# Grouping the intra-chunk levels of a gated linear attention differently in a two-layer trunk

## The chip, the cores and the metric

The kernel runs on one core of one Trainium2 chip. A core has a matrix engine (TensorE; in the profile PE, with its weight loads as PEld), three other compute engines (VectorE, DVE; ScalarE, ACT; GpSimd, POOL) and a queue engine for transfers (SyncE, SP). Each engine works through its own instructions in order, and semaphores tie the engines together. The metric is the time of one execution in microseconds (us) on the device.

## The reference, cut to what matters

The program is a trunk of two layers over 256 tokens of width 2048, all in fp32. The even layer runs two mixers side by side, HGRN2 (a gated linear recurrence with a 128 x 128 state per head, eight heads) and a gated recurrence (RG-LRU); the odd layer is an mLSTM. Each layer ends with a gated embedding. The change touches only HGRN2:

```python
w = exp(where(causal, b[:, :, :, None, :] - b[:, :, None, :, :], -inf))   # b = cumsum(log f)
attn = einsum('bhtd,bhsd,bhtsd->bhts', qc, kc, w)
o = einsum('bhtd,bhde->bhte', qc * exp(b), state) + einsum('bhts,bhse->bhte', attn, vc)
new_state = exp(b_last) * state + einsum('bhsd,bhse->bhde', kc * exp(b_last - b), vc)
```

The score of query t and key s is a sum over d of q, k and the product of all forget gates f between s and t.

## The kernel before, in words

**The frame.** The time goes into projections: the activations stand in SBUF, feature by token, split into a high and a low fp32r part (tiles "ahl" in a pool "ap" of 12 buffers), and the weights stream in from HBM. `load_half` loads 128 x 1024 weights into "raw" (5 buffers), ScalarE casts them to "whi" (line 134), VectorE subtracts to "wlo" (line 135), four buffers each. `part_tok` uses two such halves: 24 matmuls of 128 x 512, 12 for each half of the tokens, three for each block of 128 x 128 (lines 164, 165, 166: whi by high, wlo by high, whi by low). Four parts make one projection of 512 columns (`project_tok`), whose sums stand in the PSUM pool "pm", three banks.

**What sets the order.** Everything else is written as generators in lanes. In the middle of each part, after its first 12 matmuls, `pump` takes one step of every lane, and what a step issues is placed behind the matmuls issued so far; the casts and subtractions of weights have a raised priority, so that the scheduler places them ahead. One step of the attention thus comes in each part.

**The attention (`attention(g)`, two groups of four heads).** The scores in a chunk of 32 tokens are built by levels B = 1, 2, 4, 8, 16: at level B the keys of the left half of each block of 2B tokens meet the queries of the right half, each already multiplied by the gates between it and the middle. `scale(B, ...)` takes keys and queries from level B to level 2B: the right queries times the left block's total gate (line 554), the left keys times the right block's total (line 555), and the totals of the next level (line 560). The other two halves stay as they are: where the output is another tile, ScalarE copies them (lines 557, 558); where it is the same tile nothing is to be done. `level(B, ...)` issues 32 matmuls of 32 columns by 16 into a bank of the PSUM pool "px" (tag "mx", three banks), and `keep(B, ...)` writes the valid ones into C by a masked copy on VectorE (line 573). C begins as the diagonal's product (lines 582 and 586).

The steps of a group before: scaled query qf; then diagonal and level 1, and scaling 1 in place; scaling 2 into the tiles k2 and q2; levels 2 and 4, and scaling 4 in place; scaling 8 back into k and qf; levels 8 and 16; scaling 16 in place with the factors of the pairs (64 and 128 tokens); the pairs of 32 and 64 in 48 matmuls (line 642), those of 128 in four (line 647), and all of C and the pairs copied into A by ScalarE (lines 651, 652 and 654); then `read_out`, which multiplies A with the values (lines 675, 678).

Of the kernel before, what the change touches and what calls it, by code (L numbers as in the profile page):

```python
# [11 lines left out]
F32 = mybir.dt.float32  # L12
# [32 lines left out]
def trunk(ctx: ExitStack, tc: tile.TileContext, a, out):  # L45
# [433 lines left out]
    if True:  # L479
# [50 lines left out]
        def attention(g):  # L530
# [10 lines left out]
            k2 = m0.tile([P, 1024], F32, name="k2", tag="k2", bufs=1)  # L541
            q2 = m0.tile([P, 1024], F32, name="q2", tag="q2", bufs=1)
            tot = [f]

            def sides(x, B):
                x = x.rearrange("p (n two b) -> p n two b", two=2, b=B)
                return x[:, :, 0, :], x[:, :, 1, :]

            def scale(B, ko, qo, ki, qi):

                n = 512 // B
                tv = tot[0].rearrange("p (n two) -> p n two", two=2)
                (k0, k1), (q0, q1), (kl, kr), (ql, qr) = (sides(x, B) for x in (ko, qo, ki, qi))
                v.tensor_tensor(out=q1, in0=qr, in1=tv[:, :, 0:1].to_broadcast([P, n, B]), op=ALU.mult)
                v.tensor_tensor(out=k0, in0=kl, in1=tv[:, :, 1:2].to_broadcast([P, n, B]), op=ALU.mult)
                if ko is not ki:
                    s.copy(q0, ql)
                    s.copy(k1, kr)
# [5 lines left out]
            def level(B, ps, at, kk, qq):  # L564
                for c in range(8):
                    for x in range(0, P, 32):
                        o = c * P + x
                        te.matmul(at(ps, c)[x:x + 32], kk[:, o:o + 32], sides(qq[:, o:o + 32], B)[1],  # L568
                                  start=True, stop=True)

            def keep(B, src, cs=slice(0, 8)):
                n = cs.stop - cs.start
                v.copy_predicated(
                    C[:, cs].rearrange("p c (n two b) -> p c n two b", two=2, b=B)[:, :, :, 1, :],
                    lmask[B].rearrange("p (n b) -> p n b", b=B).unsqueeze(1).to_broadcast([P, n, 16 // B, B]),
                    src)

            ps = px.tile([P, 512], F32, name="mx", tag="mx")
            for c in range(8):
                for x in range(0, P, 32):  # L580
                    o = c * P + x
                    te.matmul(ps[x:x + 32, 256 + c * 32:288 + c * 32], k[:, o:o + 32], q[:, o:o + 32],
                              start=True, stop=True)
            level(1, ps, lambda ps, c: ps[:, c * 16:(c + 1) * 16], k, qf)
            t1 = scale(1, k, qf, k, qf)
            v.tensor_tensor(out=C, in0=ps[:, 256:512].rearrange("p (c t) -> p c t", c=8),
                            in1=ident32.unsqueeze(1).to_broadcast([P, 8, 32]), op=ALU.mult)
            keep(1, ps[:, 0:128].rearrange("p (c n b) -> p c n b", c=8, b=1))
            yield
            scale(2, k2, q2, k, qf)  # L590
            yield
            for a_, b_ in ((2, 4), (8, 16)):
                (ka, qa), (kb, qb) = ((k, qf), (k2, q2)) if a_ == 2 else ((k2, q2), (k, qf))
                ps = px.tile([P, 512], F32, name="mx", tag="mx")
# [12 lines left out]
            tot = tot[0]  # L607
# [8 lines left out]
            for i in (1, 0):  # L616
# [7 lines left out]
            k5 = k.rearrange("p (h two b s) -> p h two b s", two=2, b=4, s=32)  # L624
            q5 = qf.rearrange("p (h two b s) -> p h two b s", two=2, b=4, s=32)
            v.tensor_tensor(out=k64, in0=k4[:, :, 0], in1=tb[:, :, 1:2].to_broadcast([P, 8, 32]), op=ALU.mult)
# [684 lines left out]
```

## Time and profile before

| what | value |
|---|---|
| median of 3 runs | 1042.88 us |
| lowest and highest of them | 1041.94 and 1043.24 us |
| the profiled execution's own time | 1041.8 us |
| its span | 1040.0 us |
| mean granted TensorE clock | 0.997 |
| TensorE, matmuls | 1028.8 us, 99% of the span |
| VectorE | 716.6 us, 69% |
| ScalarE | 596.6 us, 57% |

All times of the trace count from the span's start and come from the one profiled execution. A row of a timeline gives start and duration in us, engine, line, operation, output and inputs, shape, and in brackets the idle time of that engine ahead of it with what ended it. Matmuls are pipelined: a row's duration overlaps with the next, so that the distance of two starts, not the duration, is what one costs. An fp32 matmul leaves two records.

### The profile page before, as it was taken

Reading aid. Unit: us, or ns where it says so; the run is one execution under the profiler, and the core shown is the slowest. Engines: PE = TensorE matmul, PEld = TensorE weight load, DVE = VectorE, ACT = ScalarE, POOL = GpSimd, SP = SyncE. Lnnn points to the kernel's source line nnn. Section 1 sums busy time; section 2 is a strip of 40 time slices with the busy share of each in tenths; the row PEclk is TensorE's granted clock in tenths of the full one; section 3 lists DMA queues with packets and bytes.
Section 4 is the critical chain, followed back from the end, with each engine's and each line's share of the span. In section 5 each row is a group of like instructions: output and inputs, shape, how many; then the busy total and the mean of one; then the engine's idle time right before and its main releaser. Section 6 shows DMA issues by size and latency. Waiting matters only on the chain.

```text
span 1040.0 us, 15509 instructions
## 1 busy us (share of the span) xinstructions
PE 1028.8 (99%) x5710; PEld 861.6 (83%) x5710; DVE 716.6 (69%) x1056; ACT 596.6 (57%) x907; POOL 157.0 (15%) x289
## 2 busy tenths in 40 slices
PE   9999999999999999999999999999999999999996
PEld 7888888888878888888889888888888888888886
DVE  6757766779876666777555658885656777666675
ACT  7665565577894354555544656866444654344553
POOL 0020110211222221032000112200001121221120
PEclk9999999999999999999999999999999999999998
DMA  9887664667788787697655678665468887787652
GB/s 339 323 270 241 216 206 164 218 189 222 243 276 260 238 264 236 205 264 258 208 189 192 224 227 263 209 211 169 167 201 229 256 270 237 222 268 239 202 183 81
DMA packets 69036, 236.02 MB, mean 227 GB/s; under 512 B 10328, under 2 KB 10720, under 8 KB 68960
## 3 DMA queue, kind: packets, MB, share of 16 engines
q1 hardware_dynamic: 55584, 197.26, 57.8%
q0 software_dynamic: 13376, 37.77, 13.4%
q8 instruction: 44, 0.72, 0.3%
q14 instruction: 32, 0.26, 0.1%
HBM read 217.16 MB, written 17.83 MB: 226 GB/s over the span
## 4 chain that ended last, share of the span: by engine, by line
PE 95%; DMA 2%; ACT 1%; DVE 0%; SPq 0%; issue 0%; DVEq 0%; ACTq 0%
PE mm L164 29%; PE mm L165 29%; PE mm L166 29%; DMA xq<-in_xT_dram 2%; PE mm L205 1%; PE mm L203 1%; PE mm L204 1%; PE mm L1164 1%; PE mm L1163 1%; PE mm L1162 1%; PE mx L568 1%; PE st L1089 0%; PE st L1088 0%; PE st L1090 0%; PE mx L675 0%; PE mx L996 0%
## 5 line engine op out<-in xcount | busy, mean ns | idle before, releaser
L135 DVE TENSOR_TENSOR wlo<-raw,whi 128x1024 fp32r<-128x1024 f32 (+2 forms) x366 | 444.2, 1220 | 253.4 <-ACT whi L134 240.9
L134 ACT CAST whi<-raw 128x1024 fp32r<-128x1024 f32 (+2 forms) x366 | 381.2, 1045 | 302.0 <-PE mm L166 253.1
L164 PE MATMUL mm<-whi,ahl 128*128 128x512 f32 x1344 | 524.2, 390 | 0.5 <-ACT uz L808 0.5
L165 PE MATMUL mm<-wlo,ahl 128*128 128x512 f32 x1344 | 523.4, 389 | 0.2
L166 PE MATMUL mm<-whi,ahl 128*128 128x512 f32 x1344 | 523.2, 389 | 0.0
L164 PEld LDWEIGHTS mm<-whi,ahl 128*128 128x128 f32 x1344 | 252.3, 188 | 52.9 <-ACT uz L808 1.0
L165 PEld LDWEIGHTS mm<-wlo,ahl 128*128 128x128 f32 x1344 | 252.3, 188 | 52.7 <-DVE wlo L135 1.2
L166 PEld LDWEIGHTS mm<-whi,ahl 128*128 128x128 f32 x1344 | 252.3, 188 | 52.7
L397 POOL DMA_DIRECT2D turned<-zt x96 | 55.5, 607 | 339.6 <-DVE zt L394 250.6
L400 POOL DMA_DIRECT2D zt<-turned x48 | 23.7, 514 | 57.2 <-DMA turned<-zt 44.5
L866 DVE SCALAR_TENSOR_TENSOR qk<-zt,prm,qk 128x255 f32<-128x255 f32 (+2 forms) x48 | 20.9, 474 | 0.7 <-ACT qk L863 0.5
L1080 POOL DMA_DIRECT2D pnr<-in_rows_dram x4 | 2.3, 566 | 125.6 <-DVE pl L1092 97.6
L247 ACT CAST ahl<-zt 128x256 fp32r<-128x256 f32 x32 | 11.7, 402 | 12.0 <-DMA zt<-turned 12.0
L205 PE MATMUL mm<-whi,ahl 128*128 128x256 f32 (+1 forms) x64 | 18.3, 287 | 0.0
L203 PE MATMUL mm<-whi,ahl 128*128 128x256 f32 (+1 forms) x64 | 18.2, 285 | 0.0
L204 PE MATMUL mm<-wlo,ahl 128*128 128x256 f32 (+1 forms) x64 | 18.2, 285 | 0.0
L1163 PE MATMUL mm<-wlo,ahl 128*128 128x256 f32 x64 | 18.1, 283 | 0.0
L1164 PE MATMUL mm<-whi,ahl 128*128 128x256 f32 x64 | 18.1, 283 | 0.0
L1162 PE MATMUL mm<-whi,ahl 128*128 128x256 f32 x64 | 18.1, 283 | 0.0
L248 DVE TENSOR_TENSOR ahl<-zt,ahl 128x256 fp32r<-128x256 f32 x32 | 12.3, 415 | 7.7 <-ACT ahl L247 7.7
L1150 POOL TENSOR_TENSOR pl<-pl,row 128x512 f32<-128x512 f32 x6 | 10.2, 1712 | 46.8 <-ACT sq L1138 46.8
L394 DVE STREAM_TRANSPOSE zt<-hq 128x512 f32<-128x512 f32 x24 | 17.0, 707 | 0.4
(309 smaller groups left out, 832.6 us busy)
## 6 DMA issues: line engine op xcount, KB each, us to landing
raw<-in_ew_dram SPq DMA_DIRECT2D x64, 512.0 KB, 5.0
raw<-in_g_dram SPq DMA_DIRECT2D x56, 512.0 KB, 5.3
raw<-in_eo_dram SPq DMA_DIRECT2D x32, 512.0 KB, 5.4
raw<-in_oqk_dram SPq DMA_DIRECT2D x32, 512.0 KB, 4.6
raw<-in_oog_dram SPq DMA_DIRECT2D x32, 512.0 KB, 4.6
raw<-in_oz_dram SPq DMA_DIRECT2D x32, 512.0 KB, 4.7
raw<-in_oo_dram SPq DMA_DIRECT2D x32, 512.0 KB, 5.4
turned<-zt POOLq DMA_DIRECT2D x96, 128.0 KB, 4.5
```

Of the source, the lines that this page charges most:

```text
L134: last["act"] = s.copy(h, r).ins
L135: last["dve"] = v.tensor_tensor(out=l, in0=r, in1=h.bitcast(F32), op=ALU.subtract).ins
L164: te.matmul(ps[hf], xh, wh, start=(k == 4 * first), stop=False)
L165: te.matmul(ps[hf], xh, wl, start=False, stop=False)
L166: last["pe"] = te.matmul(ps[hf], xl, wh, start=False, stop=(k == 4 * end + 3)).ins
L203: te.matmul(ps[hf], xh, wh, start=(k == 0), stop=False)
L204: te.matmul(ps[hf], xh, wl, start=False, stop=False)
L205: last["pe"] = te.matmul(ps[hf], xl, wh, start=False, stop=(k == KT - 1)).ins
L397: gp.dma_start(out=d.rearrange("i c (x a m) -> i (c x) a m", x=2, a=4)[:, :, k], in_=z[32 * k:32 * k + 32].rearrange("p (b m) -> p b m", b=8))
L1162: te.matmul(ps[hf], xh, wh, start=(k == 0), stop=False)
L1163: te.matmul(ps[hf], xh, wl, start=False, stop=False)
L1164: last["pe"] = te.matmul(ps[hf], xl, wh, start=False, stop=(k == KT - 1)).ins
```

## The change

`scale(B)` always writes into another tile now. The tiles of each level stand in a table `by`: levels 1 and 16 in k and qf, 2 and 32 in k2 and q2, and 4 and 8 in four new tiles of 128 x 1024 in the activations' pool "ahl". The steps become: scaling 1; scaling 2; scaling 4; then the diagonal and levels 1, 2, 4 and 8 one after another into two "mx" banks, with the masked copies of all four and scaling 8; scaling 16; the factors of the pairs; then level 16, its masked copy, and the pairs. The number of steps, matmuls and VectorE instructions is the same; each scaling issues ScalarE's two copies now, ten per group instead of four.

```diff
+            by = {1: (k, qf), 2: (k2, q2), 16: (k, qf), 32: (k2, q2)}
+            for B in (4, 8):
+                by[B] = [ap.tile([P, 1024], F32, name=f"{n}{B}", tag="ahl") for n in "kq"]
...
-            def scale(B, ko, qo, ki, qi):
-
+            def scale(B):
+
+                (ki, qi), (ko, qo) = by[B], by[2 * B]
...
-                if ko is not ki:
-                    s.copy(q0, ql)
-                    s.copy(k1, kr)
+                s.copy(q0, ql)
+                s.copy(k1, kr)
...
-            level(1, ps, lambda ps, c: ps[:, c * 16:(c + 1) * 16], k, qf)
-            t1 = scale(1, k, qf, k, qf)
-            v.tensor_tensor(out=C, in0=ps[:, 256:512].rearrange("p (c t) -> p c t", c=8),
+            scale(1)
+            t1 = tot[0]
+            yield
+            scale(2)
+            yield
+            scale(4)
+            yield
+            ps, p2 = (px.tile([P, 512], F32, name="mx", tag="mx") for _ in range(2))
...
+            found = ((1, ps, 256), (2, ps, 384), (4, p2, 0), (8, p2, 128))
+            for x in found:
+                level(*x)
+            v.tensor_tensor(out=C, in0=ps[:, 0:256].rearrange("p (c t) -> p c t", c=8),
                             in1=ident32.unsqueeze(1).to_broadcast([P, 8, 32]), op=ALU.mult)
-            keep(1, ps[:, 0:128].rearrange("p (c n b) -> p c n b", c=8, b=1))
-            yield
-            scale(2, k2, q2, k, qf)
-            yield
-            for a_, b_ in ((2, 4), (8, 16)):
-                (ka, qa), (kb, qb) = ((k, qf), (k2, q2)) if a_ == 2 else ((k2, q2), (k, qf))
-                ps = px.tile([P, 512], F32, name="mx", tag="mx")
-                level(a_, ps, lambda ps, c: ps[:, c * 16:(c + 1) * 16], ka, qa)
-                level(b_, ps, lambda ps, c: ps[:, 128 + c * 16:144 + c * 16], kb, qb)
-                if b_ == 4:
-                    scale(b_, kb, qb, kb, qb)
-                for i, B in enumerate((a_, b_)):
-                    keep(B, ps[:, i * 128:(i + 1) * 128].rearrange("p (c n b) -> p c n b", c=8, b=B))
-                yield
-                if b_ == 4:
-                    scale(8, ka, qa, kb, qb)
-                    yield
-                else:
-                    scale(b_, kb, qb, kb, qb)
+            for x in found:
+                keep(*x)
+            scale(8)
+            yield
+            scale(16)
+            yield
...
-            k4 = k.rearrange("p (c b s) -> p c b s", b=4, s=32)
-            q4 = qf.rearrange("p (c b s) -> p c b s", b=4, s=32)
+            k4 = k2.rearrange("p (c b s) -> p c b s", b=4, s=32)
+            q4 = q2.rearrange("p (c b s) -> p c b s", b=4, s=32)
...
+            ps = px.tile([P, 512], F32, name="mx", tag="mx")
+            level(16, ps, 0)
+            keep(16, ps, 0)
             banks = []
```

The order of TensorE in the first group before, the three small clumps of levels (mx from q or qf and k; a tile with a number is one of several of its letter, here k2 and q2), with the large matmuls between them left out:

```order
L166 MATMUL mm<-whi,ahl 128x512
L582 MATMUL mx<-q,k 32x32 x32
L568 MATMUL mx<-qf,k 32x16 x32
L164 MATMUL mm<-whi,ahl 128x512
...
L568 MATMUL mx<-qf,k 32x16 x32
L568 MATMUL mx<-q_1082,k_1081 32x16 x32
...
L568 MATMUL mx<-q_1082,k_1081 32x16 x32
L568 MATMUL mx<-qf,k 32x16 x32
```

And now, the one clump, and the beginning of the later one with the pairs (1084 and 1083 are the tiles of level 4, 1086 and 1085 those of level 8):

```order
L166 MATMUL mm<-whi,ahl 128x512
L592 MATMUL mx<-q,k 32x32 x32
L572 MATMUL mx<-qf,k 32x16 x32
L572 MATMUL mx<-q_1082,k_1081 32x16 x32
L572 MATMUL mx<-q_1084,k_1083 32x16 x32
L572 MATMUL mx<-q_1086,k_1085 32x16 x32
L164 MATMUL mm<-whi,ahl 128x512
...
L572 MATMUL mx<-qf,k 32x16 x32
L642 MATMUL mx<-q_1082,k_1081 32x32 x3
```

Three entries from large to small matmuls have become one, and level 16 has joined the entry of the pairs; the one clump stands one part later than the middle one of before stood.

The order of VectorE behind the second clump of the first group, before:

```order
L554 TENSOR_TENSOR q_1082<-q_1082,tot_1206 128x128x4
L555 TENSOR_TENSOR k_1081<-k_1081,tot_1206 128x128x4
L573 COPY_PREDICATED C<-cst,mx 128x64x2
L554 TENSOR_TENSOR qf<-q_1082,tot_1311 128x64x8
L573 COPY_PREDICATED C<-cst,mx 128x32x4
L555 TENSOR_TENSOR k<-k_1081,tot_1311 128x64x8
L135 TENSOR_TENSOR wlo<-raw,whi 128x1024 x2
```

And now, behind the one clump:

```order
L558 TENSOR_TENSOR qf<-q_1086,tot_1187 128x64x8
L559 TENSOR_TENSOR k<-k_1085,tot_1187 128x64x8
L596 TENSOR_TENSOR C<-mx,cst 128x256
L558 TENSOR_TENSOR q_1082<-qf,tot_1396 128x32x16
L576 COPY_PREDICATED C<-cst,mx 128x128
L559 TENSOR_TENSOR k_1081<-k,tot_1396 128x32x16
L576 COPY_PREDICATED C<-cst,mx 128x64x2
L509 TENSOR_SCALAR f<-f,omb,lb 128x256
L576 COPY_PREDICATED C<-cst,mx 128x32x4
L576 COPY_PREDICATED C<-cst,mx 128x16x8
L135 TENSOR_TENSOR wlo<-raw,whi 128x1024 x2
```

The scheduler has drawn scaling 16 up beside scaling 8, so that four products, the diagonal's and four masked copies stand between the clump and the next pair of weight halves; the products of levels 1, 2 and 4 stand ahead of the clump now.

ScalarE in the same place: the copies of scaling 8 and 16 stand in one row, behind the evacuation of a projection (uf) and ahead of the next pair of casts. Before, only the first two of the four were there, between casts.

```order
L498 ACTIVATE uf<-mm,rcr 128x512
L507 ACTIVATE k<-uf 128x256
L508 ACTIVATE f<-uf 128x256
...
L560 COPY qf<-q_1086 128x64x8
L561 COPY k<-k_1085 128x64x8
L560 COPY q_1082<-qf 128x32x16
L561 COPY k_1081<-k 128x32x16
L134 CAST whi<-raw 128x1024 x2
```

The orders of SP and POOL are the same as before.

More of the change, by code (lines that the diff above doesn't have):

```diff
@@ L562, in scale, with level @@
                 return nt
-            def level(B, ps, at, kk, qq):
+            def level(B, ps, at):
+                kk, qq = by[B]
                 for c in range(8):
@@ L567, in level, with keep @@
                         o = c * P + x
[L568 to L572, printed above, removed]
+                        te.matmul(ps[x:x + 32, at + c * 16:at + c * 16 + 16], kk[:, o:o + 32],
+                                  sides(qq[:, o:o + 32], B)[1], start=True, stop=True)
+            def keep(B, ps, at):
                 v.copy_predicated(
-                    C[:, cs].rearrange("p c (n two b) -> p c n two b", two=2, b=B)[:, :, :, 1, :],
-                    lmask[B].rearrange("p (n b) -> p n b", b=B).unsqueeze(1).to_broadcast([P, n, 16 // B, B]),
-                    src)
-            ps = px.tile([P, 512], F32, name="mx", tag="mx")
+                    C.rearrange("p c (n two b) -> p c n two b", two=2, b=B)[:, :, :, 1, :],
+                    lmask[B].rearrange("p (n b) -> p n b", b=B).unsqueeze(1).to_broadcast([P, 8, 16 // B, B]),
+                    ps[:, at:at + 128].rearrange("p (c n b) -> p c n b", c=8, b=B))
+            scale(1)
[6 more added lines that the diff above has]
+            ps, p2 = (px.tile([P, 512], F32, name="mx", tag="mx") for _ in range(2))
             for c in range(8):
@@ L581, in attention @@
                     o = c * P + x
-                    te.matmul(ps[x:x + 32, 256 + c * 32:288 + c * 32], k[:, o:o + 32], q[:, o:o + 32],
-                              start=True, stop=True)
-            level(1, ps, lambda ps, c: ps[:, c * 16:(c + 1) * 16], k, qf)
-            t1 = scale(1, k, qf, k, qf)
-            v.tensor_tensor(out=C, in0=ps[:, 256:512].rearrange("p (c t) -> p c t", c=8),
+                    te.matmul(ps[x:x + 32, c * 32:c * 32 + 32], k[:, o:o + 32], q[:, o:o + 32], start=True, stop=True)
+            found = ((1, ps, 256), (2, ps, 384), (4, p2, 0), (8, p2, 128))
+            for x in found:
+                level(*x)
+            v.tensor_tensor(out=C, in0=ps[:, 0:256].rearrange("p (c t) -> p c t", c=8),
                             in1=ident32.unsqueeze(1).to_broadcast([P, 8, 32]), op=ALU.mult)
-            keep(1, ps[:, 0:128].rearrange("p (c n b) -> p c n b", c=8, b=1))
+            for x in found:
+                keep(*x)
+            scale(8)
             yield
-            scale(2, k2, q2, k, qf)
+            scale(16)
             yield
-            for a_, b_ in ((2, 4), (8, 16)):
-                (ka, qa), (kb, qb) = ((k, qf), (k2, q2)) if a_ == 2 else ((k2, q2), (k, qf))
-                ps = px.tile([P, 512], F32, name="mx", tag="mx")
-                level(a_, ps, lambda ps, c: ps[:, c * 16:(c + 1) * 16], ka, qa)
-                level(b_, ps, lambda ps, c: ps[:, 128 + c * 16:144 + c * 16], kb, qb)
-                if b_ == 4:
-                    scale(b_, kb, qb, kb, qb)
-                for i, B in enumerate((a_, b_)):
-                    keep(B, ps[:, i * 128:(i + 1) * 128].rearrange("p (c n b) -> p c n b", c=8, b=B))
-                yield
-                if b_ == 4:
-                    scale(8, ka, qa, kb, qb)
-                    yield
-                else:
-                    scale(b_, kb, qb, kb, qb)
             tot = tot[0]
@@ L621, in attention @@
             kx, qx = (f[:, i * 512:(i + 1) * 512] for i in range(2))
[L622 to L625 removed]
+            k4 = k2.rearrange("p (c b s) -> p c b s", b=4, s=32)
+            q4 = q2.rearrange("p (c b s) -> p c b s", b=4, s=32)
+            k5 = k2.rearrange("p (h two b s) -> p h two b s", two=2, b=4, s=32)
+            q5 = q2.rearrange("p (h two b s) -> p h two b s", two=2, b=4, s=32)
             v.tensor_tensor(out=k64, in0=k4[:, :, 0], in1=tb[:, :, 1:2].to_broadcast([P, 8, 32]), op=ALU.mult)
```

## The prediction

> **What bounds the kernel now.** I read the page first: busy shares, slices and the chain of waits.
>
> ```profile
> span 1040.0 us, 15509 instructions
> PE 1028.8 (99%) x5710; PEld 861.6 (83%) x5710; DVE 716.6 (69%) x1056; ACT 596.6 (57%) x907; POOL 157.0 (15%) x289
> PE 95%; DMA 2%; ACT 1%; DVE 0%; SPq 0%; issue 0%; DVEq 0%; ACTq 0%
> ```
>
> The chain that ended last is TensorE for 95% of the span. The other engines only matter where TensorE waits for them, so I asked next for TensorE's own waits, over the whole program:
>
> ```profile
> engine line waited for: us in total, times, longest us
> PE st L94 <- POOL ones L91: 1.0, 1, 1.0
> PE mm L164 <- ACT uz L808: 0.5, 1, 0.5
> ```
>
> Two waits, 1.5 us, neither in the attention. So whatever the change does to VectorE and ScalarE is worth nothing unless it makes a new wait on TensorE, and what it can give is TensorE time inside the attention's own stretch (108 to 222 us). The view of the tile "mx" says what is issued there:
>
> ```profile
> L568 PE MATMUL mx<-qf,k x384: 182/183/203, 108.4 to 208.6; 128*32 128x16 f32 x192
> L568 PE MATMUL mx<-q,k x256: 182/183/203, 120.7 to 208.0; 128*32 128x16 f32 x128
> L582 PE MATMUL mx<-q,k x128: 196/196/217, 107.8 to 183.4; 128*32 128x32 f32 x128
>   issue: 2.8, 8
> ...
> L568 PEld LDWEIGHTS mx<-qf,k 128*32 128x32 f32 x384 | 3.9, 108 | 0.7 <-issue 0.7
> ```
>
> The levels' matmuls have 384 + 256 = 640 records, which is 2 groups x 5 levels x 32 x 2: each fp32 matmul leaves two records. They come in clumps between the large matmuls: four per group, eight in all. Eight is also the number of idle pieces of 0.35 us that the view puts down to "issue", that is, to nothing it can name; the last row, from the groups by line, shows that it is the weight loads (PEld) that sat idle so. One clump of the first group, levels 2 and 4, from the timeline of TensorE (start, duration):
>
> ```profile
> 119.37 0.39 PE L164 MATMUL mm<-whi,ahl 128*128 128x512 f32 x1
> 119.59 0.39 PE L165 MATMUL mm<-wlo,ahl 128*128 128x512 f32 x1
> 119.82 0.39 PE L166 MATMUL mm<-whi,ahl 128*128 128x512 f32 x1
> 120.14 0.70 PE L568 MATMUL mx<-qf,k 128*32 128x16 f32 x62
> ...
> 120.71 0.70 PE L568 MATMUL mx<-q,k 128*32 128x16 f32 x62
> 121.34 0.50 PE L164 MATMUL mm<-whi,ahl 128*128 128x512 f32 x1
> 121.67 0.40 PE L165 MATMUL mm<-wlo,ahl 128*128 128x512 f32 x1
> 121.91 0.39 PE L166 MATMUL mm<-whi,ahl 128*128 128x512 f32 x1
> ```
>
> Large matmuls start 0.23 us apart (119.37 to 119.82 is two steps of 0.225, 121.67 to 121.91 one of 0.24). A set of 32 small ones takes 0.57 us from the start of one set to the next (120.14 to 120.71).
>
> **The change part by part.** *TensorE.* Per group it issues the same matmuls: the diagonal's 32, five levels of 32, 48 and 4 of the larger pairs. Only their grouping moves: clumps of (diagonal, 1), (2, 4), (8, 16), (pairs) become (diagonal, 1, 2, 4, 8) and (16, pairs). Two clumps fewer per group, four in all. What does a clump cost beyond its matmuls? From 119.82 to 121.67, the last large matmul before to the second after, are 1.85 us; without the clump they would be two steps, 0.46; the two sets are 1.14. What is left is 1.85 - 0.46 - 1.14 = 0.25 us: 0.09 on the way in (0.32 instead of 0.23), 0.06 in the last set (0.63 instead of 0.57) and 0.10 on the way out (0.33 instead of 0.23). Four clumps fewer: **-1.0 us**. Bounds: nothing at all, if this fixed piece belongs to the sets and comes along with them, and above, if I believe the records' 0.35 us of idle on the way in instead of the 0.09 between starts, 0.35 + 0.16 = 0.51 per clump, 2.0 us. I take 0.25, because the ends of matmuls in this profile are modelled and only the starts are measured.
>
> [...]
>
> *ScalarE and VectorE.* Scaling into other tiles instead of in place adds two ScalarE copies at levels 1, 4 and 16: six per group, twelve in all. The nearest rows are the copies of the levels 2 and 8:
>
> ```profile
> 122.24 0.63 ACT L557 COPY qf<-q 128x512 f32<-128x512 f32 x1 [3.62 <-DVE q L554]
> 122.84 0.63 ACT L558 COPY k<-k 128x512 f32<-128x512 f32 x1
> 123.37 2.12 ACT L134 CAST whi<-raw 128x1024 fp32r<-128x1024 f32 x2
> ```
>
> About 0.6 us each, 12 x 0.6 = 7.2 us of ScalarE. That engine is at 57% and TensorE waits for it once in the program, far from here, so I cost it at nothing, as long as the casts of the weights (whi) and the subtractions (wlo) behind these steps come in time. This is the cover, and I check it where it is thinnest. VectorE's instructions stay the same in number; they move. In the old first clumps VectorE worked behind TensorE; after the second clump (TensorE back at 121.34) it did this:
>
> ```profile
> 121.46 0.69 DVE L554 TENSOR_TENSOR q<-q,tot 128x512 f32<-128x512 f32 x1 [1.44 <-PE mx L568]
> 122.07 0.69 DVE L555 TENSOR_TENSOR k<-k,tot 128x512 f32<-128x512 f32 x1
> 122.67 0.45 DVE L573 COPY_PREDICATED C<-cst,mx 128x128 f32<-128x128 uint32 x1
> 122.90 0.73 DVE L554 TENSOR_TENSOR qf<-q,tot 128x512 f32<-128x512 f32 x1
> 123.55 0.29 DVE L573 COPY_PREDICATED C<-cst,mx 128x128 f32<-128x128 uint32 x1
> 123.74 0.69 DVE L555 TENSOR_TENSOR k<-k,tot 128x512 f32<-128x512 f32 x1
> 124.45 2.36 DVE L135 TENSOR_TENSOR wlo<-raw,whi 128x1024 fp32r<-128x1024 f32 x2
> 126.73 0.41 DVE L509 TENSOR_SCALAR f<-f,omb,lb 128x256 f32<-128x256 f32 x1
> ```
>
> So 0.6 us per product, 0.2 per masked copy, 3.0 in all, and then the pair of weight halves. TensorE needs this pair when the rest of the present part (12 matmuls) and the next part (24), whose halves are already in the other two of the four buffers, are through: 36 x 0.23 = 8.3 us after the clump, at 129.6. The pair was ready at 126.8: 2.8 us to spare. In the changed kernel the block behind the long clump holds four products (2.4), the diagonal's product, four masked copies (0.8) and in the first group one L509 (0.3). The diagonal's product is bounded by its two rows here:
>
> ```profile
> 111.29 0.42 DVE L586 TENSOR_TENSOR C<-mx,cst 128x256 f32<-128x256 f32 x1
> 111.62 0.68 DVE L554 TENSOR_TENSOR q<-qf,tot 128x512 f32<-128x512 f32 x1
> ```
>
> 0.33 from start to start. Sum 2.4 + 0.3 + 0.8 + 0.3 = 3.8 us, then the pair, 2.4: ready 6.2 us after the clump against 8.3 needed, **2.1 us to spare**. ScalarE has four copies there instead of two, 2.4 us, then the pair of casts, 2.1: done at 4.5, in time for the subtractions. The scalings of levels 1, 2 and 4 now wait for no clump and run ahead of it; the inputs of level 8 are ready two weight parts before it. The long clump itself lasts 5 x 0.57 + 0.25 = 3.1 us, and with TensorE busy in it, nothing starves.
>
> *The closing step.* Level 16, its masked copy and the diagonal's last copies into A now stand in the step of the pairs. Rows of before, from the timelines of ScalarE and TensorE:
>
> ```profile
> 137.67 1.65 ACT L654 COPY A<-C 32x256 f32<-32x256 f32 x4
> 145.74 2.25 ACT L651 COPY A<-mx 32x384 f32<-32x384 f32 x6 [2.49 <-PE mx L642]
> 148.01 0.59 ACT L652 COPY Ac<-st 128x512 f32<-128x512 f32 x1
> 152.86 0.72 PE L675 MATMUL mx<-vt,A 128*128 128x128 f32 x5
> ```
>
> The four copies of C were done 7 us before the pairs' matmuls; now they follow level 16, so the 1.65 us come into this step and A is complete up to 1.7 us later than the 148.6 of before. The reading matmul stands at 152.9, 4.3 us later: 2.6 us to spare, cost nothing. The third "mx" bank that level 16 takes is free there, since the long clump's two are read out three steps earlier. The tiles in the pool of the activations cost nothing either: 12 buffers, 8 held by the input's splits, the four others idle until the first y, and four are taken. No DMA is added or moved; the queues of SP and POOL have the same order.
>
> Sum: 1041.8 us (the profiled execution, span 1040.0 and 1.8 around it) - 1.0 + 0 = 1040.8. This execution lies 1.1 below the median of the runs shown, 1042.88; against that median the forecast is **1041.9 us**, no change that a measurement can tell (about 0.2%, 2.1 us either way).
>
> **The rivals.** *A, slower: the block behind the long clump starves TensorE.* VectorE and ScalarE depend on each other in it: VectorE's products into the level-32 inputs read what ScalarE copies, and ScalarE's last copies read what VectorE multiplies. If they take turns rather than overlap, four copies (2.4) and the block (3.8) add up to 6.2 us, and if the casts (2.1) and subtractions (2.4) come after one another behind them, the pair is ready at 10.7 instead of 8.3: 2.4 us per group, 4.8 - 1.0 = +3.8, **1046.7**. It decides from 2.1 us of added delay on. For it: VectorE did wait on clumps before (1.44 above), and it is full (10.00 of 10) behind the second group's third clump:
>
> ```profile
> 210.00:220.00 10.00, 10.00 (x58) 8.03 (x59) 10.00 (x19) 6.83 (x10) 2.00 (x4) 1.00 0.74 232
> ```
>
> (columns: the stretch, its length, then busy time and instructions of PE, PEld, DVE, ACT and POOL, then clock, DMA share and GB/s). Against it: the rows show both engines working side by side in the same block (122.24 beside 122.07), and no wait of TensorE there.
>
> [...]
>
> *B, the read-out waits.* In the second group level 16's masked copy is queued on VectorE behind the convolution's products and two pairs of weights. If VectorE, full as the row above shows, comes there late by two pairs, 4.7 us, the 2.6 us of cover are gone and the reading matmul waits 2.1, once: +2.1 - 1.0, **1044.0**. Against it: six of A's copies wait for the pairs' matmuls anyway, and the blocks that filled this stretch are partly moved ahead of it.
>
> *C, faster: the clump's fixed piece is what the idle records say,* 0.51 us: 4 x 0.51 = 2.0, **1040.8**, on the edge of what can be told. For it: eight times 0.35 us of idle in the view. Against it: the start times.
>
> *That the change does less than it says,* all clumps kept, would be 1042.9, and is out: the order shows two per group.
>
> **How the numbers follow.** Forecast 0.66, A 0.14, B 0.05, C 0.15. The forecast's own range is 1041.3 to 1042.9 with the bound of nothing gained, and about 0.5 us of the runs' own spread below it. To hold 8 in 10 I go down past C to 1040.4 and up to 1045.0, which holds B and the milder half of A. Faster by over 0.2%: two thirds of C and a few hundredths of the forecast, 0.14. Slower: A and a little of B, 0.15. Same: 0.71.
>
> **What would show it.** In the changed profile: two clumps per group on TensorE, the first some 3.1 us long with five sets of 32 at 0.57; "issue" idle of "mx" four times 0.35 fewer; TensorE's waits still two, of 1.5 us; TensorE's share of the chain unchanged; ScalarE's busy time up by 7 us. A wait of TensorE on wlo or whi some 8 us behind the long clump would show A, one of L675 on A would show B. A span shorter by 2 us or more, with the same matmuls, would prove the 0.25 too small.

## The result, and the profile after

The changed kernel takes **1059.41 us** (median of 5 runs) beside 1042.88 of the kernel before in the same measurement (1041.61 to 1043.24): a ratio of **1.0159, 95% interval 1.0147 to 1.0171**, 16.5 us slower. Forecast were 1041.9 us with a range of 1040.4 to 1045.0: the measured time lies 14.4 us above its upper end. Four of the five runs lie at 1057.27 to 1062.16; the fifth, 1744.53 at a mean granted clock of 0.556, was disturbed and is left out of the ratio (the median of the four is 1058.67). The profiled execution took 1057.93 us.

The page of the changed kernel, its span, its engines' busy time, the chain of waits and one line of the transfer queues:

```profile
span 1056.2 us, 15538 instructions
PE 1033.1 (98%) x5710; PEld 865.2 (82%) x5710; DVE 716.7 (68%) x1056; ACT 603.9 (57%) x919; POOL 156.9 (15%) x289
PE 94%; DMA 2%; issue 1%; ACT 1%; DVE 0%; SPq 0%; DVEq 0%; ACTq 0%
q8 instruction: 44, 0.72, 0.3%
```

Span +16.2 us with the same 5710 matmul records. TensorE's busy time rose by only 4.3 us, so most of what was lost is idle time. The waits of TensorE (line, what it waited for, us in total, times, longest) name no engine for it:

```profile
PE mx L572 <- issue: 8.6, 3, 3.8
PE st L647 <- issue: 2.8, 1, 2.8
PE st L94 <- POOL ones L91: 1.0, 1, 1.0
PE mm L164 <- ACT uz L808: 0.5, 1, 0.5
PE mm L165 <- DVE wlo L135: 0.5, 1, 0.5
```

The last three sum to 2.0 us, against 1.5 before. New are four pieces of "issue", 11.4 us: time in which TensorE had nothing to wait for that the profile can see, and still did nothing. The timeline of TensorE shows where; first the long clump of the first group:

```profile
124.09 0.73 PE L592 MATMUL mx<-q,k 128*32 128x32 f32 x62
...
124.67 0.67 PE L572 MATMUL mx<-qf,k 128*32 128x16 f32 x60
...
125.20 0.79 PE L572 MATMUL mx<-q,k 128*32 128x16 f32 x71
129.17 1.19 PE L572 MATMUL mx<-q,k 128*32 128x16 f32 x119 [3.18 <-issue]
130.29 0.63 PE L164 MATMUL mm<-whi,ahl 128*128 128x512 f32 x1
130.72 0.63 PE L165 MATMUL mm<-wlo,ahl 128*128 128x512 f32 x1
...
134.04 0.39 PE L164 MATMUL mm<-whi,ahl 128*128 128x512 f32 x1
134.27 0.40 PE L165 MATMUL mm<-wlo,ahl 128*128 128x512 f32 x1
```

The clump runs at the pace of before (0.58 us from the first set's start to the second's, 0.53 to the third's), stops with 119 of its 320 records to go, and goes on 3.18 us later. 201 records are done then, an odd number, and a matmul leaves two: TensorE stands still **inside one fp32 matmul**, where no operand can be missing that was there for its first half. And the large matmuls behind it stand 0.43 us apart instead of 0.23 until 134.0. The second group stops twice in its long clump, and once more in its clump of pairs:

```profile
204.51 0.53 PE L572 MATMUL mx<-q,k 128*32 128x16 f32 x39
208.81 1.80 PE L572 MATMUL mx<-q,k 128*32 128x16 f32 x128 [3.78 <-issue]
212.27 0.52 PE L572 MATMUL mx<-q,k 128*32 128x16 f32 x23 [1.66 <-issue]
...
232.88 0.38 PE L647 MATMUL st<-f 128*128 128x128 f32 x1
236.02 1.62 PE L647 MATMUL st<-f 128*128 128x128 f32 x7 [2.76 <-issue]
```

That the pace is halved behind the idle time is seen in the granted clock (the last number but two of each row; the same stretches had 1.00 before):

```profile
130.00:140.00 10.00, 10.00 (x78) 8.12 (x67) 5.81 (x16) 4.86 (x8) 0.28 (x1) 0.83 0.32 96
200.00:210.00 10.00, 6.22 (x282) 5.27 (x284) 5.17 (x8) 5.16 (x11) 0.00 (x0) 0.95 0.53 180
210.00:220.00 10.00, 8.34 (x96) 6.79 (x88) 5.02 (x9) 4.12 (x6) 0.00 (x0) 0.71 0.09 29
230.00:240.00 10.00, 7.24 (x179) 6.10 (x178) 2.00 (x4) 4.37 (x11) 0.00 (x0) 0.83 0.48 136
```

**Where the 16.2 us went**, from these timelines: idle 3.18 + 3.78 + 1.66 + 2.76 = 11.4; 22 large matmuls at the halved clock, 9.5 from start to start (130.29 to 134.04, 212.72 to 215.86, 237.29 to 239.88) against 0.23 each, 4.4; the small matmuls behind the stalls, slowed in the same way, some 1.4 (the 128 records at 208.81 take 1.80 where two sets, 128 records, take 1.14; the rest in the other three pieces). Sum 17.2; less the 1.0 that four clumps fewer were to save, 16.2.

**Theories.** Three were set against each other.

- *P (pages)*: an assumption, which the experiments test: TensorE's instructions come in pieces of 256, one piece ahead. A small fp32 matmul is four instructions (two weight loads and two matmul records: 640 of each for the 320 matmuls of the levels), a large one two (one of each: 1344 and 1344 on line 164). A stretch of small ones eats a piece in 128 records, some 1.1 us; a piece of large ones lasts 128 x 0.23 = 29 us. If a clump crosses one border of pieces and comes to the next before the following piece has landed, TensorE stops at that border. ("Border" stands below for the place where one piece ends and the next begins.) The line of the queue q8 above fits in size: 0.72 MB for TensorE's 11,420 loads and matmuls is 63 bytes each, and 44 packets are 260 instructions each. Counted in the order of issue (in the changed kernel the long clumps begin at instruction 1068 and 2668, of 640 instructions each, the closing ones at 1852 and 3452, of 336), the four stalls lie ahead of number 1470, 3006, 3262 and 3774: all leave 190 when divided by 256. In the kernel before no clump has over 256 instructions.
- *D (data)*: the new tiles, the copies or the order of the scalings make the clump wait in a way that the profile does not show.
- *T (throttle)*: the long row of small matmuls itself loses the clock, and the stalls go with it.

### The profile page after: what moved, and what is told of

It reads as the page before. It is cut to its first block, busy times and chain, and to the rows that moved or that the text cites. A ratio compares the mean times of both kernels' runs of the same rounds, so it can differ in the third digit from the quotient of the medians.

```text
span 1056.2 us, 15538 instructions
## 1 busy us (share of the span) xinstructions
PE 1033.1 (98%) x5710; PEld 865.2 (82%) x5710; DVE 716.7 (68%) x1056; ACT 603.9 (57%) x919; POOL 156.9 (15%) x289
## 2 busy tenths in 40 slices
DMA packets 69036, 236.02 MB, mean 223 GB/s; under 512 B 10328, under 2 KB 10720, under 8 KB 68960
## 4 chain that ended last, share of the span: by engine, by line
PE 94%; DMA 2%; issue 1%; ACT 1%; DVE 0%; SPq 0%; DVEq 0%; ACTq 0%
PE mm L164 28%; PE mm L165 28%; PE mm L166 28%; DMA xq<-in_xT_dram 2%; PE mm L205 1%; PE mm L203 1%; PE mm L204 1%; PE mm L1164 1%; PE mm L1163 1%; PE mm L1162 1%; PE mx L572 1%; PE st L1090 0%; PE st L1089 0%; PE st L1088 0%; PE mx L675 0%
## 5 line engine op out<-in xcount | busy, mean ns | idle before, releaser
L1150 POOL TENSOR_TENSOR pl<-pl,row 128x512 f32<-128x512 f32 x6 | 10.2, 1712 | 49.6 <-ACT sq L1138 49.6
L400 POOL DMA_DIRECT2D u<-turned x24 | 11.8, 511 | 35.5 <-DMA turned<-num 22.6
L400 POOL DMA_DIRECT2D uf<-turned x24 | 11.9, 507 | 25.6 <-DMA turned<-zt 19.3
```

Of the source, the lines that this page charges most:

```text
L400: gp.dma_start(out=dst[32 * c:32 * c + 32], in_=d[:, c])
```

## The experiments

P makes a prediction of a rare kind: it says after how many matmul records of which clump TensorE stops. So most of the runs shift the borders against the clumps, or cut the clumps differently. For each, the positions were worked out beforehand.

**1. The change with its borders shifted.** 48 small matmuls on constants, into a bank that is free then. They are more work than the program needs, and stand in the trace behind the first three matmuls of the first projection (18.86 us); nothing else differs from the changed kernel.

```diff
+    fill = pst.tile([P, 512], F32, name="fill", tag="st")
+    for i in range(48):
+        te.matmul(fill[0:32, 0:16], ones[:, 0:32], ones[:, 0:16], start=True, stop=True)
     rp0 = small(2, "rp0")
```

> The changed kernel with 48 small matmuls more (ones by ones, 32x16, into a spare bank that nobody reads) in TensorE's idle start, ahead of the first projection; nothing else. Theory P (pages): TensorE's instruction stream comes in pieces of 256 instructions with one piece ahead; a small fp32 matmul is 4 instructions, a large one 2. The four stalls of the changed kernel all stand at the same place modulo 256. 192 instructions more move the borders against the clumps: one stall per long clump (after 233 of 320 records in the first group, 201 in the second) and none in the clumps of the pairs, 2 instead of 4: about 1051 us. Theory D (data or buffers: the later sets wait for copies, scalings or a bank): nothing of that is moved, four stalls, 1059. Theory T (the clock throttle reacts to a long row of small matmuls): the rows are as long as before, four stalls, 1059.

Measured: 1052.79 us (1052.19 to 1053.8), ratio to before 1.0096 [1.0079, 1.0113], **6.6 us less than the changed kernel with more work in it**. Its timeline has two stalls, none in the clumps of pairs:

```profile
128.79 1.08 PE L575 MATMUL mx<-q,k 128*32 128x16 f32 x103
133.21 0.92 PE L575 MATMUL mx<-q,k 128*32 128x16 f32 x87 [3.34 <-issue]
...
212.10 1.51 PE L575 MATMUL mx<-q,k 128*32 128x16 f32 x119 [3.06 <-issue]
```

320 - 87 = 233 and 320 - 119 = 201 records into their clumps, as P said to the record. D and T have no reason to move a stall by work that was done 100 us earlier.

**2. Shifted elsewhere.** The same edit with `range(15)`.

> The changed kernel with 15 such small matmuls (60 instructions) at the start. P: six stalls: first group's long clump after 171 and 299 records, its clump of the pairs after 163 records, second group's long clump after 139 and 267, its clump of the pairs after 131: about 1067 us. D and T: as the changed kernel, four stalls, 1059.

Measured: 1057.83 us (1055.18 to 1059.51), ratio 1.0144 [1.0125, 1.0162]; some 9 us less than P's sum. Four stalls of the six are there, each at its record: 4.01 us after 171 and 1.55 after 299 in the first long clump, 2.53 after 163 in its clump of pairs, and one in the second long clump:

```profile
213.99 1.37 PE L575 MATMUL mx<-q,k 128*32 128x16 f32 x137
217.98 0.87 PE L575 MATMUL mx<-q,k 128*32 128x16 f32 x53 [2.62 <-issue]
```

Missing are those at 139 in that clump (it ran through to 320 - 53 = 267) and at 131 in the last clump of pairs. Exactly there the first border lies just behind the clump's beginning, 22 and 6 instructions in. So P needs an addition: the fetch runs ahead of what TensorE executes (in the changed kernel transfers of q8 begin up to 5.8 us before their border is executed), so that a border so early in the clump was passed while the large matmuls still ran, and the next piece had its time. Experiment 7 estimates how far ahead.

**3. The kernel before, with a longer clump.** Levels 2 and 4 are issued twice, the second time into the free half of the bank: 128 matmuls in one clump (512 instructions) where there were 64. In-place scaling, tiles and copies are those of before; the second results are not used.

```diff
                 level(b_, ps, lambda ps, c: ps[:, 128 + c * 16:144 + c * 16], kb, qb)
                 if b_ == 4:
+                    level(a_, ps, lambda ps, c: ps[:, 256 + c * 16:272 + c * 16], ka, qa)
+                    level(b_, ps, lambda ps, c: ps[:, 384 + c * 16:400 + c * 16], kb, qb)
+                if b_ == 4:
                     scale(b_, kb, qb, kb, qb)
```

> The kernel before, with the sets of levels 2 and 4 issued a second time into the free half of their own bank right behind (64 matmuls more per group, their results unused). Same inputs, same waits, in-place scaling. P: 512 instructions in a row must cross two borders: one stall per group, after 225 of 256 records in the first and 193 in the second: 2 x 1.14 for the matmuls and some 5 each for stall and slow clock, about 1055 us. D: all inputs are there, only the matmuls' own 2.3 us: 1045. T: 2.3 us of small matmuls in a row where 3.1 was too long; a stall or none, at no fixed place.

Measured: 1057.99 us (1057.45 to 1058.74), ratio 1.0148 [1.0133, 1.0163]. The timeline has one stall per group, of 4.86 and 4.11 us, 31 and 63 records before the clumps' ends (256 - 31 = 225, 256 - 63 = 193, as P said). The span is 17.0 us longer: 9.0 idle and 2.3 for four sets more, which leaves 5.7 for the halved clock behind the stalls. So the stall needs nothing of the change but the length of the clump: D falls. The time is 3 us over P's figure, which took the changed kernel's shorter stalls.

**4. What the filler costs.** The kernel before with the 48 small matmuls of experiment 1.

> The kernel before, with the 48 small matmuls at the start. Control for the shift itself: P says that 256 instructions in a row never need more than the piece at hand and the next one, wherever the border falls: 1042.9, as before; the 48 matmuls run while the first transfers are awaited and cost nothing. D and T say the same.

Measured: 1044.58 us (1044.16 to 1045.6), ratio 1.0023 [1.0014, 1.0033], and no stall: this shift of the borders does nothing where no clump is over 256 instructions. The 1.7 us over the expectation are the filler itself, whose place I had chosen badly:

```profile
17.67 3.21 PE L357 MATMUL fill<-ones 128*32 128x16 f32 x96
20.81 0.50 PE L164 MATMUL mm<-whi,ahl 128*128 128x512 f32 x1
```

3.14 us from start to start for 48 matmuls, 65 ns each, where a set of 32 in a clump takes 0.57, 18 ns each. TensorE was not idle there, but in its first projection. All 48 write one place of 32 output rows by 16 columns, `fill[0:32, 0:16]`; the sets go round the four blocks of 32 rows (the "row groups" of the expectations) and write each place once.

**5. All of the change but the long clumps.** Tiles, table and twelve copies as in the change; five clumps per group of at most 256 instructions: diagonal and 1; 2 and 4; 8; 16; pairs.

```diff
-            scale(4)
-            yield
...
-            for x in found:
-                level(*x)
+            level(1, ps, 256)
...
+            keep(1, ps, 256)
+            scale(4)
+            yield
...
+            level(2, ps, 0)
+            level(4, ps, 128)
+            keep(2, ps, 0)
+            keep(4, ps, 128)
             scale(8)
             yield
+            ps = px.tile([P, 512], F32, name="mx", tag="mx")
+            level(8, ps, 0)
+            keep(8, ps, 0)
             scale(16)
```

(level 16 follows one step later, in the step of the pairs' factors.)

> The changed kernel's scaling into other tiles, its tiles in the activations' pool and all its copies, but the sets apart: diagonal and 1 in the step of scaling 4, 2 and 4 in the next, 8 in the next, 16 in the step of the factors, then the pairs: five clumps per group of at most 256 instructions. P: no stall; one clump more per group than before at 0.25 us, 1043.4. D: the copies and buffers are all there, so most of the loss stays, 1055 to 1059. T: rows of at most 1.4 us, no stall, 1043.

Measured: 1043.52 us (1042.65 to 1044.45), ratio 1.0014 [1.0005, 1.0023]; no stall, clock 0.997, and ScalarE at 603.8 us of busy time as in the change. Of the changed kernel's +16.5 us, 1.4 are left when only the grouping is taken back, of which P counted 0.5 for one clump more per group. D, which had 1055 to 1059, is out for good.

**6. Level 16 apart.** The change with level 16 and its masked copy one step earlier; the clump of pairs has 208 instructions again, the long clump is as in the change.

```diff
             scale(16)
             yield
+            ps = px.tile([P, 512], F32, name="mx", tag="mx")
+            level(16, ps, 0)
+            keep(16, ps, 0)
...
-            ps = px.tile([P, 512], F32, name="mx", tag="mx")
-            level(16, ps, 0)
-            keep(16, ps, 0)
             banks = []
```

> The changed kernel with level 16 one step earlier, apart from the pairs; the long clump as it is. P: the long clumps stall as before (after 201 records; after 169 and 297), the pairs' clump of 208 instructions does not: the second group's 2.8 us and some 1.3 of slow clock go, one clump per group more costs 0.5: about 1056. D: what waits in the long clump waits still; 1059 or 1056. T: 1056.

Measured: 1054.24 us (1053.81 to 1055.75), ratio 1.0120 [1.0106, 1.0133]. The three stalls of the long clumps stay at their places (3.03 us; 3.95 and 2.10), the one in the pairs is gone, and with it 4.1 us (1.0159 less 1.0120; the intervals leave 2 to 6). By the middle value one stall of 2.8 us cost more than its idle time; the interval alone does not show that, the granted clock of 0.83 behind this stall (230 to 240, above) does.

**7. How far the fetch is ahead.** The change with eight small matmuls at the start, spread over the four blocks of 32 rows this time. The borders now lie 50 and 34 instructions behind the beginnings of the second group's two clumps.

```diff
+    for i in range(8):
+        x, o = 32 * (i % 4), 16 * (i // 4)
+        te.matmul(fill[x:x + 32, o:o + 16], ones[:, 0:32], ones[:, 0:16], start=True, stop=True)
```

> The changed kernel with 8 small matmuls more at the start, spread over the four row groups (32 instructions more in TensorE's stream; by the long clump's 8.4 ns each some 0.1 us, and 0.25 for the clump). Theory P (pages of 256 instructions, one ahead): borders now fall 114 instructions into the first group's long clump, 98 into its pairs' clump, 50 and 34 into the second group's. P without a lead of the fetch: stalls after 185 records of the first long clump (some 3.5 us) and after 313 (1.6), none in the first pairs' clump (its second border would be 354 in, it has 336), after 153 records of the second long clump (3.8 us) and 281 (1.6), and after 145 of the second pairs' clump (2.7): 13.2 us of idle, time some 1061. P with a lead (the fetch runs some 45 to 66 instructions ahead of what TensorE executes, as the 15-filler run suggested, whose borders 22 and 6 instructions in caused no stall): the second pairs' clump stalls by 0 to 1.5 us in place of 2.7, and the second long clump's first stall is shorter than 3.8 where the lead is above 50. Time 1054 to 1059. A theory without pages has the changed kernel's 1059 and its idle at the changed kernel's places (201, 169 and 297 records, 161 in the second pairs' clump).

Measured: 1059.21 us (1058.22 to 1060.58), ratio 1.0160 [1.0144, 1.0175], as slow as the change itself, but with five stalls at the five records named: 3.23 and 1.55 us in the first long clump, then

```profile
213.80 1.28 PE L576 MATMUL mx<-q,k 128*32 128x16 f32 x128 [3.63 <-issue]
217.25 0.73 PE L576 MATMUL mx<-q,k 128*32 128x16 f32 x39 [2.17 <-issue]
...
239.72 0.22 PE L646 MATMUL mx<-tot,k 128*32 128x32 f32 x1 [1.32 <-issue]
```

The last, with its border 34 instructions in, is half of the 2.76 us (66 in, the change) and 2.53 (70 in, experiment 2) in clumps of pairs. One large instruction lasts 0.23 / 2 = 0.115 us. A fetch some 46 instructions ahead passes a border at 34 twelve large instructions early, 1.4 us, which leaves 1.3 of 2.7; one at 22 twenty-four early, 2.8 us, which leaves nothing; and at 50 it gains nothing (3.63). This is an estimate, fitted to these four, and likely somewhat low: among large matmuls the trace of experiment 8 has transfers of a piece that begin 6.0 us before the border is executed, which at 0.115 us is 52 instructions.

**8. Three clumps whose borders fall well.** Diagonal with levels 1 and 2 (384 instructions), 4 with 8 (256), 16 with the pairs (336); tiles and copies of the change; 51 small matmuls at the start, chosen so that no clump comes to a second border.

```diff
+            level(1, ps, 256)
+            level(2, ps, 384)
...
+            keep(1, ps, 256)
+            keep(2, ps, 384)
+            scale(4)
+            yield
             scale(8)
             yield
             scale(16)
             yield
+            ps = px.tile([P, 512], F32, name="mx", tag="mx")
+            level(4, ps, 0)
+            level(8, ps, 128)
+            keep(4, ps, 0)
+            keep(8, ps, 128)
```

> The changed kernel with three clumps per group (diagonal, 1 and 2; 4 and 8; 16 and the pairs: 384, 256 and 336 instructions) and 51 small matmuls at the start, a number chosen so that no clump crosses two borders. P: no stall although rows of 384 and 336 instructions stand there, one clump per group less than before: 1042.9 - 0.5 = 1042.4. D: scalings and copies as in the changed kernel, slower than before by several us. T: rows of 1.7 and 2.2 us; the latter stalled in the changed kernel, so it should here, by some 4 us.

Measured: 1044.35 us (1043.15 to 1045.07), ratio 1.0019 [1.0010, 1.0029]; no stall, clock 0.998. It is 1.9 over P's figure; the filler, all at one place as in experiment 4, took 3.3 us here. Beside experiment 4's 1044.58 nothing is lost. Clumps of 384 and 336 instructions are harmless where the second border falls outside, so length alone does not do it, and T falls. The order in time says the same: in the changed kernel the granted clock is still full in the first stall and halved behind it (columns as above):

```profile
126.00:129.10 3.10, 0.00 (x0) 0.00 (x0) 3.10 (x8) 2.17 (x5) 0.00 (x0) 1.00 0.27 102
130.50:133.90 3.40, 3.40 (x9) 2.65 (x9) 0.51 (x2) 0.81 (x1) 0.00 (x0) 0.50 0.00 0
```

**9. Fewer fillers, and a miss.** Three clumps as in 8, the first two of them a step earlier, and 11 spread fillers.

> The out-of-place scaling of the change in three clumps per group (diagonal with levels 1 and 2, one step after the first scaling; levels 4 and 8 three steps later; level 16 with the pairs) and 11 small matmuls more at the start, spread over the four row groups, so that borders fall 198, 182 and 86 instructions into the first group's clumps and 134, 118 and 22 into the second's. P with a lead of the fetch: no stall anywhere, no half clock; two clumps fewer than before (0.5 us less) and one short filler clump more (0.35): time 1042.0 to 1042.9, before's 1042.1 to 1042.9 beside it. P without a lead: one stall of some 2.7 us after 139 records of the second pairs' clump and half clock behind it, 1046 to 1047. Theory D (the new buffers, the copies or the order of the scaling cost time): above 1048.

Measured: 1050.8 us (1048.83 to 1050.99), ratio 1.0079 [1.0066, 1.0091]. P's two figures are missed; the number is one that D had named (above 1048). The timeline decides: it shows two stalls, and both stand **outside** the small matmuls:

```profile
147.12 1.16 PE L655 MATMUL st<-f 128*128 128x128 f32 x8
148.03 0.47 PE L164 MATMUL mm<-whi,ahl 128*128 128x512 f32 x1
148.34 0.39 PE L165 MATMUL mm<-wlo,ahl 128*128 128x512 f32 x1
148.57 0.39 PE L166 MATMUL mm<-whi,ahl 128*128 128x512 f32 x1
151.03 0.39 PE L164 MATMUL mm<-whi,ahl 128*128 128x512 f32 x1 [2.07 <-issue]
...
193.00 0.50 PE L164 MATMUL mm<-whi,ahl 128*128 128x512 f32 x1
193.34 0.39 PE L165 MATMUL mm<-wlo,ahl 128*128 128x512 f32 x1
193.57 0.40 PE L166 MATMUL mm<-whi,ahl 128*128 128x512 f32 x1
198.16 0.80 PE L164 MATMUL mm<-whi,ahl 128*128 128x512 f32 x1 [4.19 <-issue]
```

TensorE stops after three large matmuls, six instructions, in both. The first clump of pairs has 336 instructions and its borders at 86 and 342; the second group's first clump 384, and its borders at 134 and 390: each second border is six instructions behind the clump's end. I had counted borders inside the clumps only. By P the piece is still under way when the clump has ended, so the count must take the time between two borders, whatever is issued there. Here TensorE stops at ordinary large matmuls, so operands of the small ones cannot be what it waits for. The border 22 instructions into the last clump does not cause a stall of 2.7 us, as P without a lead had it, but it does cause a small one, at the next border (230.15 us, remainder 190 again):

```profile
PE mx L650 <- issue: 0.3, 1, 0.3
```

**10. The best grouping found.** Experiment 8 with its 51 fillers spread over the four blocks of 32 rows (edit as in 7).

> The three clumps per group of the 51-filler run (borders 246, 230, 182 and 182, 166, 118 instructions into the clumps, the next one at least 38 instructions behind each clump's end), with the 51 small matmuls of the filler spread over the four row groups in place of one. Theory P: no stall, no half clock. In the earlier run the filler took 3.4 us at one row group; spread it takes 51 x 8.4 ns and 0.25 = some 0.7 us, so 2 to 2.7 us less than that run's 1044.35: 1041.7 to 1042.4, beside 1042.1 to 1042.9 of before, which is no difference that can be measured. If what is left of the change (copies, tiles, order of the scaling) costs time by itself: 1043 and more.

Measured: 1042.16 us (1041.33 to 1042.45, 11 runs) beside 1042.01 of before, ratio **0.9995 [0.9986, 1.0005]**: no difference. All of TensorE's waits are

```profile
PE st L94 <- POOL ones L91: 1.0, 1, 1.0
PE mm L164 <- ACT uz L816: 0.5, 1, 0.5
PE mm L165 <- DVE wlo L135: 0.2, 1, 0.2
```

Experiment 8 took 2.2 us more, and only the filler differs. The spread fillers add 1.07 us (my 8.4 ns each were those of one record; a matmul is two). So with three clumps per group in place of two, and the borders placed, none of the change's loss is left, and what fewer clumps give back is too small to be measured. No version here beats the kernel before.

**What is shown, what is argued.** Over the changed kernel and these runs there are 22 stalls of over 1.2 us in this stretch, and all 22 stand at an instruction that leaves 190 when divided by 256, at small fp32 matmuls, at those of 128 x 128 and at large ones alike; experiments 4, 5, 8 and 10, whose borders lie apart, have none. A 23rd, of 0.33 us in experiment 9, has the same remainder. The unit of 256 and the place are shown.

That TensorE waits for the piece itself can be read from the queue q8, whose every transfer the trace keeps with its time. In each run it carries one transfer of 16,384 bytes for each border (44 in the kernel before, in the changed one and in experiment 5, 45 in experiments 4 and 10). In the stretch of the first stall there is one:

```profile
q8 instruction: 1, 0.02, 6.0%
```

(126.5 to 127.8 us; 6.0% of 16 engines for 1.3 us are 1.25 us of transfer; from 127.8 to 129.2 no queue moves anything.) For the four stalls of the changed kernel, in us:

| border passed | transfer behind it | TensorE goes on at the next border |
|---|---|---|
| 124.7 | 126.54 to 127.78 | 129.17 |
| 203.8 | 206.21 to 207.22 | 208.81 |
| 208.81 | 209.84 to 210.81 | 212.27 |
| 231.0 | 233.47 to 234.62 | 236.02 |

In all 23 stalls TensorE goes on 1.2 to 1.7 us after the end of the transfer that followed the border before. At the other borders of the 12 traces, some 500, that transfer had ended at least 1.7 us before, save one at 1.5. No transfer begins more than 6.0 us before its border is executed, among large matmuls 52 instructions, so never two pieces ahead. One piece ahead, and no more, is thus shown as well. The moment at which a piece is asked for is not on record, only the transfer.

## Why the prediction was wrong

**The step that failed** is the one that costs TensorE's part: "Only their grouping moves", with the sentence on the long clump, "lasts 5 x 0.57 + 0.25 = 3.1 us, and with TensorE busy in it, nothing starves". I took a matmul's price to be the same wherever it stands, and asked only whether TensorE would be fed with data. It was the instructions that did not come. The unlisted term was +17.2 us: 11.4 of stalls and 5.8 of halved clock (4.4 on large matmuls, 1.4 on small ones). None of the three rivals holds it, so the range had no side where it could lie.

**What in the profile of before spoke of it.** The sum of the trace's rows had it: 640 records for five levels of two groups, as many weight loads, so a set of 32 is 128 instructions, and a clump 256 or 208. I counted records and time and never instructions per time: 128 instructions in 0.57 us against 128 in 128 / 2 x 0.23 = 14.7 us of large matmuls, a demand 26 times as high, for 3 us instead of 1.1. The eight pieces of 0.35 us "issue" of the weight loads were no clue to this: they come with each entry, border or not. In the changed kernel they are there beside the stalls, four fewer as forecast (groups by line; last two numbers: idle us and its reason):

```profile
L572 PEld LDWEIGHTS mx<-q,k 128*32 128x32 f32 x384 | 4.4, 124 | 8.9 <-issue 8.9
L572 PEld LDWEIGHTS mx<-qf,k 128*32 128x32 f32 x256 | 2.6, 109 | 0.7 <-issue 0.7
L592 PEld LDWEIGHTS mx<-q,k 128*32 128x32 f32 x128 | 1.3, 110 | 0.7 <-issue 0.7
```

**-1.0 us for four clumps fewer**: not contradicted, not proved. The ledger of the result section closes with it (17.2 - 1.0 = 16.2), but its own pieces are uncertain by some tenths. One clump more per group (experiment 5) measured +1.4 us [0.5, 2.4] where 0.25 each gives 0.5; two fewer with 1.07 of filler (experiment 10) measured -0.5 [-1.5, +0.5], where it gives +0.6. Both lie at the edge of the intervals; rival C's 0.51 per clump gives 1.0 and 0.0, inside both. So 0.25 may be too small, and the measurements cannot say by how much.

**Copies and masked copies at nothing**: right. ScalarE rose by 7.3 us (forecast 7.2), VectorE by 0.1, and experiments 5 and 10, with all of these, lose 1.4 [0.5, 2.4] and nothing that can be measured.

**A, the block behind the long clump starves TensorE**: not seen. TensorE waits for wlo once, 0.5 us. In the changed kernel the stall gave the other engines three more microseconds, so it proves little; in experiment 10, with three clumps and no stall, the wait is 0.2. The unstalled long clump itself, five sets with five evacuations behind them, could not be built: 640 instructions cross at least two borders wherever they begin.

**B, the read-out waits for A**: did not happen; the line of the read-out (L675) is in no wait of TensorE.

**"What would show it"**: two clumps per group, yes; first clump of 3.1 us with five sets, no (6.2 us from its first start to the next large matmul: 124.09 to 130.29); "issue" of the weight loads four times 0.35 fewer, yes; TensorE's share of the chain unchanged, nearly (94% beside 95); TensorE's waits still two, no. The list asked for a wait on wlo or on A, not for a wait on nothing; the row "issue" was the one to watch.

## What to carry to other kernels

When small matmuls are moved together, count their instructions between two borders, not only their time: here TensorE stood still where it passed one border and came to the next sooner than some 4 to 6 us later, and the halved clock behind the stalls added about half of the idle time again (5.8 to 11.4 in the change, 5.7 to 9.0 in experiment 3). Rows of up to one piece, with 24 or more large matmuls between them, had no stall in the kernel before and in experiments 4 and 5, though in 5 one piece came only some 0.3 us before it would have been missed (1.7 us ahead of its border, where restarts follow after 1.2 to 1.7); longer rows were a matter of luck, which any edit earlier in the program can turn. Where "issue" stands as a releaser on the engine that sets the end, ask for the distance of the stalls in instructions before looking for data.

## What the runs showed of the hardware

- TensorE's instructions came in pieces of 256 (23 stalls of 23 at one remainder; one transfer of 16,384 bytes for each border), one piece ahead (each transfer begins at most 6.0 us before its border is executed, 5.8 in the kernel before and in the changed one). From the execution of the first border, placed by its record at the clump's pace, to the restart at the second it took 4.4 to 5.0 us in the changed kernel (73 records behind 124.09, at 124.75, to 129.17) and 3.9 to 6.3 over all runs, the borders at 22 and 34 instructions left out. Of this the transfer itself takes 0.9 to 1.3 us and the time from its end to the restart 1.2 to 1.7; what varies is the time before it begins, 1.6 to 3.9 us. Where a second stall followed at once on a first, the transfer began after 1.0 to 1.7 us, and the whole took 3.5 us in four of five cases (208.81 to 212.27) and 4.0 in the fifth. That the difference is the other transfers' traffic fits the last but one column of the windows (0.09 in 210 to 220), and was not tried.
- The fetch ran some 50 instructions ahead of the execution: an estimate, from stalls of 0 and 0.33, 1.32 and 2.5 to 2.8 us with the border 22, 34 and 66 to 70 instructions into the clump (some 46), and from transfers that begin up to 6.0 us before their border, 52 instructions of 0.115 us.
- The granted clock fell to half at stalls of 2.53 us and more (2.53, 2.62, 2.76, 3.03 and above), and did not at 1.32 (experiment 7) and 2.07 (experiment 9, clock 1.00 from 120 to 170); second stalls that followed at once on another are left out here. Each halved stretch in this part lasted 3.4 us (130.5 to 133.9 and 236.3 to 239.7 in the change), 6.8 (209.0 to 215.8 there) or 10.2 (129.4 to 139.6 in experiment 2). The large matmuls in it stood 0.43 us apart. Where between 2.07 and 2.53 us the step lies, and what sets it, was not tried.
- 48 fp32 matmuls that all write one place of 32 rows by 16 columns took 3.14 us, 65 ns each; 51 spread over the four blocks of 32 rows, each with a place of its own, took 1.0, 19 ns each. Whether the block or the place makes the difference was not tried.
